# Start addresses of the split activations in a one-core transformer layer

## Chip, core and metric

One core of one Trainium2 chip. The metric is the device time of one execution in microseconds. The kernel before has a median of 2149.63 us over three runs (2149.45 to 2150.16).

## What is computed

The reference is one layer of a conformer-like network for a prompt of 256 tokens and a sample of 32 tokens, width 2048:

```python
def conformer_layer(x, mix, lp):
    x = x + 0.5 * swiglu(rmsnorm(x, lp['norm_ffn1']), lp['w_ffn1_in'], lp['w_ffn1_out'])
    y, state = mix(rmsnorm(x, lp['norm_mix']))
    x = x + y
    x = x + 0.5 * swiglu(rmsnorm(x, lp['norm_ffn2']), lp['w_ffn2_in'], lp['w_ffn2_out'])
    return rmsnorm(x, lp['norm_final']), state
```

`swiglu` projects to two times 43 x 128 columns, multiplies the silu of one half with the other, and projects back to 2048. `mix` projects to queries, keys, values and gates (`w_in`), runs a gated linear attention, a differential attention with a cache and an attention to a memory of 256 rows, and joins the three with `w_o`. All values are 32-bit floats, and so are the results: the new activations, the keys and values, and the state.

## The kernel before

All 288 tokens (256 and 32) are handled together and lie along the free dimension; channels lie on the 128 partitions. An activation of 2048 channels is thus 16 blocks of 128 x 288. The weights stream through the core once, in chunks of at most 512 KB, and each chunk is the stationary operand of TensorE.

To keep the precision of 32-bit floats with TensorE's faster 32-bit type (`float32r`), both operands are split. `split` has ScalarE (ACT) round a value to the fast type, the high part, and VectorE (DVE) subtract it, which leaves the low part. A product is then three matmuls: high weight by high activation, high weight by low activation, low weight by high activation. Weights are split chunk by chunk into the ring tiles wh and wl (`split_chunk`), four buffers each. Activations are split once per stage: the normed input into uh and ul (`prep_u`, `gsplit`), 16 blocks each, and the hidden values of the feed-forward into hh and hl, 22 blocks each, since a feed-forward is worked in two halves of 22 and 21 hidden blocks (`HALVES`).

`gemm` (line 271) is the loop that nearly all of the time goes to. For each chunk of up to four 128-row blocks it takes two column blocks of 128, and runs first all products with the high weight part, then all with the low part:

```python
for j in range(nk):
    xh, xl = xs(k + j)
    if part == 0:
        mm(o, wh[:, j, cs], xh, ci == 0 and j == 0, False)
        mm(o, wh[:, j, cs], xl, False, False)
    else:
        mm(o, wl[:, j, cs], xh, False, ci == nchunk - 1 and j == nk - 1)
```

So a chunk of four blocks is 24 matmuls, and the moving operand of each, `xh` or `xl`, is one block of 288 words per partition. All matmuls pass through one helper, line 83; which operand is meant is read from the tiles' names. `consume` (called in `gemm`) splits the weights three chunks ahead and starts loads six ahead, and between chunks `side` gives small pieces of attention work to the engines. The order on each engine is the order in which the program writes the instructions.

The stages in time: the memory's keys and values (`mem_group`, where the tiles mTh and mTl borrow the places of hh and hl), the first feed-forward (names ending in a), the projections of `mix` and the attentions, `w_o`, and the second feed-forward (names ending in b).

In the kernel before, the tiles uh, ul, hh, hl have rows of `NS` = 320 words, of which the first `NT` = 288 are used. 320 words are 1280 bytes, 5 x 256, so all blocks of a tile start at the same address modulo 256 bytes; in the layout of this program that is 32 for all four tiles. The blocks of wh and wl, 128 words wide, also all start at 32 modulo 256. The attention outputs that meet `w_o` (cdh, cdl, gch, gcl, from a pool of four-block tiles) have no padding: their blocks follow each other at 288 words, 1152 bytes, and so start at 32 and 160 in turn.

Of the kernel before, what the change touches and what calls it, by code (L numbers as in the profile page):

```python
# [11 lines left out]
F32R = mybir.dt.float32r  # L12
# [7 lines left out]
P = 128  # L20
NT = 288
NS = 320
D = 2048
KB = 16
# [16 lines left out]
def hybrid_step_kernel(  # L41
# [11 lines left out]
    def pool(name, bufs=1, **kw):  # L53
        return ctx.enter_context(tc.tile_pool(name=name, bufs=bufs, **kw))

    const = pool("const")
# [13 lines left out]
    def s1(name):  # L70
        return ps1.tile([P, 512], F32, tag="s1", name=name)
# [4 lines left out]
    def sm(name):  # L76
        return smp.tile([P, 32], F32, tag="sm", name=name)

    def sq2(name):
        return sqp.tile([P, 2, NT], F32, tag="sq", name=name)  # L80

    def mm(out, lhsT, rhs, start=True, stop=True):
        pe.matmul(out, lhsT, rhs, start=start, stop=stop)  # L83
# [5 lines left out]
    def tt(out, a, b, op):  # L89
        dve.tensor_tensor(out, a, b, op=op)  # L90

    def mul(out, a, b):
        dve.tensor_tensor(out, a, b, op=ALU.mult)  # L93
# [4 lines left out]
    def stt(out, a, s, b, op0, op1):  # L98
        dve.scalar_tensor_tensor(out, a, s, b, op0=op0, op1=op1)

    def split(hi, lo, src):
        act.copy(hi, src)  # L102
        tt(lo, src, hi.bitcast(F32), ALU.subtract)

    def gscale(out, src, g):
        act.activation(out, src, AF.Copy, scale=g)

    def gsplit(hi, lo, src, g):
        gscale(hi, src, g)
        stt(lo, src, g, hi.bitcast(F32), ALU.mult, ALU.subtract)  # L110

    def exp_tables():
        act.preload_act_table_set(ACT_SET)
# [11 lines left out]
    def kparts(n):  # L125
        return [4] * (n // 4) + ([n % 4] if n % 4 else [])
# [88 lines left out]
    def consume():  # L215
        i = nxt[2]
        nxt[2] += 1
        a = AHEAD if i >= 6 else 2
        splits_to(i + a)
        loads_to(i + a + 3)  # L220
        return chunks[i][2], halved.pop(i)
# [3 lines left out]
    class Thread:  # L225
        def __init__(self, lag):
            self.q, self.lag, self.ready = deque(), lag, 0
# [32 lines left out]
    def side(most=2):  # L260
        for t in threads:
            if most and t.can():
                t.step()
                most -= 1

    def need(mark):
        while mark not in done:
            t = next(t for t in threads if any(x[1] == mark for x in t.q))
            t.step()

    def gemm(nchunk, xs, nblk=2):

        ps = psm.tile([P, 2, 512], F32, tag="m", name=f"m{nxt[2]}")
        k = 0
        for ci in range(nchunk):
            nk, (wh, wl) = consume()
            for part in range(2):
                for b in range(nblk):
                    cs = slice(b * P, (b + 1) * P)
                    o = ps[:, b, :NT]  # L280
# [7 lines that stand above are left out]
            k += nk  # L288
            if ci < nchunk - 1:
                side()  # L290
        return ps

    fstack = [None]

    def open_ffn():
# [53 lines left out]
    x_res = const.tile([P, KB, NT], F32, name="x_res")  # L349
    G = const.tile([P, G_N], F32, name="G")  # L350
    lam = const.tile([P, 1], F32, name="lam")
    uh = const.tile([P, KB, NS], F32R, name="uh")[:, :, :NT]
    ul = const.tile([P, KB, NS], F32R, name="ul")[:, :, :NT]
    acc = const.tile([P, NT], F32, name="acc")
    dkc = const.tile([P, 4, P], F32, name="dkc")
    dvc = const.tile([P, 512], F32, name="dvc")
# [7 lines left out]
    def gcol(i):  # L364
        return G[:, i:i + 1]
# [28 lines left out]
    def prep_sq(i):  # L394

        sq = sq2("sq")
        act.activation(sq, x_res[:, 2 * i:2 * i + 2, :], AF.Square)
        if fresh[0]:
            tt(acc, sq[:, 0, :], sq[:, 1, :], ALU.add)
            fresh[0] = False  # L400
        else:
            for j in range(2):
                tt(acc, acc, sq[:, j, :], ALU.add)

    def prep_u(i, g0):
        for b in (2 * i, 2 * i + 1):
            gsplit(uh[:, b, :], ul[:, b, :], x_res[:, b, :], gcol(g0 + b))

    def later_R(name):

# [6 lines left out]
    def Rb(n):  # L417
        return acc.unsqueeze(1).to_broadcast([P, n, NT])


    hp = fstack[0][1]
    mTh = hp.tile([P, 22, NS], F32R, tag="hh", name="mTh").rearrange("p a t -> p (a t)")[:, :4096]
    mTl = hp.tile([P, 22, NS], F32R, tag="hl", name="mTl").rearrange("p a t -> p (a t)")[:, :4096]
    mTh = mTh.rearrange("p (k m) -> p k m", m=256)
    mTl = mTl.rearrange("p (k m) -> p k m", m=256)
    mss = sm("mss")
    mrs = sm("mrs")

# [25 lines left out]
    def x_step(i):  # L454
        half, o = divmod(i, 4)
        ps = s2(f"xt{i}")
        for b in range(2):
            for t, (t0, n) in enumerate(TT):
                c = (2 * o + b) * P
                tr(ps[:, b, t0:t0 + P], xtiles[half, t][:, c:c + P])  # L460
        act.copy(x_res[:, 2 * i:2 * i + 2, :], ps[:, :, :NT])
        prep_u(i, G_F1)
        prep_sq(i)
# [230 lines left out]
    def ffn(tag, mark, g_next, final=False):  # L694
        hp, fp = fstack[0][1], fstack[0][2]

        def ft(nm, bufs):
            return fp.tile([P, 2, NT], F32, tag=nm, bufs=bufs, name=f"{nm}_{tag}")

        def u(k):  # L700
            return uh[:, k, :], ul[:, k, :]

        for half, (a, b) in enumerate(HALVES):
            hh = hp.tile([P, 22, NS], F32R, tag="hh", name=f"hh{tag}{half}")[:, :, :NT]
            hl = hp.tile([P, 22, NS], F32R, tag="hl", name=f"hl{tag}{half}")[:, :, :NT]
            f = a
            while f < b:
                pair = f + 1 < b
                n = 2 if pair else 1
                ps = gemm(4, u)  # L710
                need(mark)
                gs = ft("gs", 1)[:, :n]
                sg = ft("sg", 2)[:, :n]
                mul(gs, ps[:, :n, :NT], Rb(n))
                act.activation(gs, gs, AF.Silu)  # L715
                mul(sg, gs, Rb(n))
                if pair:
                    side()
                    ps = gemm(4, u)
                    up = ps[:, :2, :NT]  # L720
                else:
                    up = ps[:, 1:2, :NT]
                hm = ft("hm", 1)[:, :n]
                mul(hm, up, sg)
                split(hh[:, f - a:f - a + n, :], hl[:, f - a:f - a + n, :], hm)
                f += n
                if f == NF:
                    exp_tables()
                side()
            for g in range(8):  # L730
                ps = gemm(len(kparts(b - a)), lambda k: (hh[:, k, :], hl[:, k, :]))
                xs = x_res[:, 2 * g:2 * g + 2, :]
                if final and half == 1 and g == 7:
                    sq = sq2("sql")
                    last_sq.append(sq)
                    for j in range(2):
                        stt(xs[:, j, :], ps[:, j, :NT], 0.5, xs[:, j, :], ALU.mult, ALU.add)
                        act.activation(sq[:, j, :], xs[:, j, :], AF.Square)
                else:
                    stt(xs, ps[:, :, :NT], 0.5, xs, ALU.mult, ALU.add)  # L740
                if half == 1:
                    if final:
                        final_pair(g)
                    else:
                        prep_sq(g)
                        prep_u(g, g_next)
                side()

    ffn("a", "R_ffn1", G_MIX)
    need("prep")  # L750
    close_ffn()
# [422 lines left out]
    later_R("mix")  # L1174

    def u(k):
        return uh[:, k, :], ul[:, k, :]

    for kind, c0, g in MIX:
        if kind == "glr":  # L1180
            ps = psm.tile([P, 2, 512], F32, tag="m", name="mglr")
# [9 lines left out]
            side()  # L1191
            continue
        ps = gemm(4, u)
        need("R_mix")
        pv = ps[:, :, :NT]
# [65 lines left out]
    for half in range(2):  # L1261
        if half == 1:
            need("gla")
        for g in range(8):
            if half == 0:
                ps = gemm(2, lambda k: (cdh[:, k, :], cdl[:, k, :]))
            else:
                ps = gemm(2, lambda k: tuple(a[:, k % 4, :] for a in M["cat", k // 4]))
# [45 lines left out]

    yr = sm("yr")
    ffn("b", "R_ffn2", None, final=True)
    ps = s1("yss")
    for j in range(2):
# [6 lines left out]
    for k, (hf, t, parts) in enumerate(((0, 0, 2), (0, 1, 1), (0, 2, 1), (1, 2, 1), (1, 0, 1), (1, 1, 1))):  # L1325
        rows = slice(0, P) if t < 2 else slice(96, P)
        dst = y_prompt[0, t * P:(t + 1) * P] if t < 2 else y_sample[0]
        n = 1024 // parts
# [66 lines left out]
```

## Time and profile before

| what | value |
|---|---|
| median of 3 runs | 2149.63 us (2149.45 to 2150.16) |
| the profiled execution's own time | 2149.8 us |
| its span, first to last instruction | 2148.0 us |
| mean granted TensorE clock | 0.996 |
| TensorE busy | 2133.2 us, 16,014 matmuls |
| VectorE, ScalarE, GpSimd busy | 1116.0, 866.0, 2.6 us |
| read from HBM | 345.59 MB |

The profile is one execution, taken by the hardware profiler. The page lists busy time by engine, the span in 40 slices, the DMA queues, the chain of work that ended last, and groups of like instructions with their count, busy time and mean duration. PE stands for TensorE's matmuls, PEld for its weight loads, DVE for VectorE, ACT for ScalarE. Matmuls are pipelined: one has a duration of about 294 ns in the records while the next starts long before it ends, so their pace is read from start to start, in the timeline or by counting them in a window.

### The profile page before, as it was taken

What the parts mean: (1) busy time and instruction counts of PE and PEld (TensorE: products, weight loads), DVE (VectorE), ACT (ScalarE), POOL (GpSimd) and SP (SyncE); (2) the same over time, 40 slices, a digit from 0 to 9 for tenths busy, and PEclk for the clock granted to TensorE, in tenths of its full rate; (3) what the DMA queues carried; (4) which work ended last, traced back from release to release, by engine and by line L of the source; (5) the groups of instructions that cost most, each with busy time, mean ns of one, the idle gap of its engine ahead of it and who ended that gap; (6) DMA issues with size and microseconds to landing.
All of it is one profiled execution on the core that took longest, in us unless ns stands there. A gap on an engine that the chain in (4) does not pass through costs nothing.

```text
span 2148.0 us, 37526 instructions
## 1 busy us (share of the span) xinstructions
PE 2133.2 (99%) x16014; PEld 2105.7 (98%) x16014; DVE 1116.0 (52%) x1318; ACT 866.0 (40%) x1113; POOL 2.6 (0%) x8
## 2 busy tenths in 40 slices
PE   9999999999999999999999999999999999999997
PEld 7999999999999999999999999999999999999997
DVE  6754444444554455554665666544544445445443
ACT  7644333333333344433544345333333333333443
POOL 0000000000000000000000000000000000000000
PEclk9999999999999999999999999999999999999998
DMA  8566555555555545554455345555555555555553
GB/s 261 177 182 189 178 166 173 171 163 172 162 168 170 166 155 166 178 151 135 121 147 154 121 151 166 168 170 168 162 167 165 169 167 166 171 167 163 160 161 117
DMA packets 351555, 353.75 MB, mean 165 GB/s; under 512 B 14112, under 2 KB 343324, under 8 KB 351388
## 3 DMA queue, kind: packets, MB, share of 16 engines
q1 hardware_dynamic: 351388, 351.36, 53.6%
q8 instruction: 125, 2.05, 0.4%
q14 instruction: 42, 0.34, 0.0%
HBM read 345.59 MB, written 5.64 MB: 164 GB/s over the span
## 4 chain that ended last, share of the span: by engine, by line
PE 98%; DMA 0%; ACT 0%; DVE 0%; SPq 0%; issue 0%; ACTq 0%; DVEq 0%
PE m L83 93%; PE mm L83 2%; PE go L83 1%; DMA ws<-in_w_mem_kv_dram 0%; PE do L83 0%; PE mo L83 0%; PE xt L87 0%; PE gK L83 0%; PE msc L83 0%; PE dsc L83 0%; PE sums L83 0%; PE yt L87 0%; PE mt L87 0%; PE hs_dq L83 0%; PE hs_mq L83 0%; PE gKs L83 0%
## 5 line engine op out<-in xcount | busy, mean ns | idle before, releaser
L90 DVE TENSOR_TENSOR wl<-ws,wh 128x1024 fp32r<-128x1024 f32 (+2 forms) x665 | 781.5, 1190 | 665.1 <-ACT wh L102 635.7
L102 ACT CAST wh<-ws 128x1024 fp32r<-128x1024 f32 (+2 forms) x665 | 665.3, 1018 | 658.6 <-PE m L83 527.5
L83 PE MATMUL m<-uh,wh 128*128 128x288 f32 x3392 | 913.5, 297 | 0.0
L83 PE MATMUL m<-ul,wh 128*128 128x288 f32 x3392 | 908.2, 294 | 0.0
L83 PEld LDWEIGHTS m<-uh,wh 128*128 128x128 f32 x3392 | 637.9, 188 | 2.9 <-issue 1.8
L83 PEld LDWEIGHTS m<-ul,wh 128*128 128x128 f32 x3392 | 638.5, 188 | 0.3
L83 PE MATMUL m<-uh,wl 128*128 128x288 f32 x3392 | 515.8, 294 | 0.0
L83 PEld LDWEIGHTS m<-uh,wl 128*128 128x128 f32 x3392 | 470.8, 188 | 0.0
L83 PE MATMUL m<-hhb,wh 128*128 128x288 f32 x688 | 184.7, 295 | 0.0
L83 PE MATMUL m<-hha,wh 128*128 128x288 f32 x688 | 184.3, 295 | 0.0
L83 PE MATMUL m<-hlb,wh 128*128 128x288 f32 x688 | 184.2, 294 | 0.0
L83 PE MATMUL m<-hla,wh 128*128 128x288 f32 x688 | 184.0, 293 | 0.0
L83 PEld LDWEIGHTS m<-hla,wh 128*128 128x128 f32 x688 | 129.1, 188 | 0.0
L83 PEld LDWEIGHTS m<-hlb,wh 128*128 128x128 f32 x688 | 129.1, 188 | 0.0
L83 PEld LDWEIGHTS m<-hhb,wh 128*128 128x128 f32 x688 | 129.1, 188 | 0.0
L83 PEld LDWEIGHTS m<-hha,wh 128*128 128x128 f32 x688 | 129.0, 188 | 0.0
L83 PE MATMUL m<-hha,wl 128*128 128x288 f32 x688 | 106.2, 294 | 0.0
L83 PE MATMUL m<-hhb,wl 128*128 128x288 f32 x688 | 106.1, 294 | 0.0
L83 PEld LDWEIGHTS m<-hha,wl 128*128 128x128 f32 x688 | 96.0, 188 | 0.0
L83 PEld LDWEIGHTS m<-hhb,wl 128*128 128x128 f32 x688 | 95.9, 188 | 0.0
L715 ACT ACTIVATE gs_b<-gs_b 128x576 f32<-128x576 f32 (+1 forms) x22 | 14.8, 674 | 84.6 <-DVE gs_b L93 84.6
L102 ACT CAST hhb<-hm_b 128x576 fp32r<-128x576 f32 (+1 forms) x22 | 14.6, 663 | 83.2 <-DVE hm_b L93 83.2
(282 smaller groups left out, 1180.1 us busy)
## 6 DMA issues: line engine op xcount, KB each, us to landing
ws<-in_w_ffn_in_dram SPq DMA_DIRECT2D x336, 512.0 KB, 4.2
ws<-in_w_ffn_out_dram SPq DMA_DIRECT2D x160, 512.0 KB, 3.5
ws<-in_w_in_dram SPq DMA_DIRECT2D x80, 512.0 KB, 3.7
ws<-in_w_o_dram SPq DMA_DIRECT2D x32, 512.0 KB, 3.5
ws<-in_w_mem_kv_dram SPq DMA_DIRECT2D x15, 512.0 KB, 5.7
ws<-in_w_ffn_out_dram SPq DMA_DIRECT2D x16, 256.0 KB, 2.8
ws<-in_w_ffn_in_dram SPq DMA_DIRECT2D x16, 256.0 KB, 3.2
x<-in_x_prompt_dram SPq DMA_DIRECT2D x4, 512.0 KB, 7.3
```

The lines of the kernel that those rows point to most:

```text
L83: pe.matmul(out, lhsT, rhs, start=start, stop=stop)
L90: dve.tensor_tensor(out, a, b, op=op)
L102: act.copy(hi, src)
L715: act.activation(gs, gs, AF.Silu)
```

## The change

The rows stay 320 words apart, but every group of four blocks is shifted by a number of words of its own. A small class holds a tile with 64 spare words and a list of shifts, one for each four blocks: block k starts at k x 320 + shift[k // 4]. `at` gives one block, `pair` two neighbours of one group.

uh and ul become one tile of 32 blocks, in which four high blocks are followed by the four low blocks of the same rows. Both get the same shift: 1, 2, 58 and 62 words for blocks 0 to 3, 4 to 7, 8 to 11 and 12 to 15. On top of the tile's own start, 32 modulo 256 bytes, that is 36, 40, 8 and 24. hh and hl stay two tiles, with shifts of 20, 28, 36, 44, 48 and 52 words for their six groups (the last has two blocks, or one in the second half): 112, 144, 176, 208, 224 and 240. Each tile grows by 64 words, 256 bytes. mTh and mTl keep the start of their tile.

```diff
+    class Blocks:
+
+        def __init__(self, pool_, n, shifts, name, **kw):
+            self.t, self.s = pool_.tile([P, n * NS + 64], F32R, name=name, **kw), shifts
+
+        def at(self, k):
+            o = k * NS + self.s[k // 4]
+            return self.t[:, o:o + NT]
+
+        def pair(self, k, n):
+            assert k // 4 == (k + n - 1) // 4
+            o = k * NS + self.s[k // 4]
+            return self.t[:, o:o + n * NT + (n - 1) * (NS - NT)] if n == 1 else \
+                self.t[:, o:o + n * NS].rearrange("p (k t) -> p k t", t=NS)[:, :, :NT]
+
+    U_SHIFT, H_SHIFT = (1, 2, 58, 62), (20, 28, 36, 44, 48, 52)
...
-    uh = const.tile([P, KB, NS], F32R, name="uh")[:, :, :NT]
-    ul = const.tile([P, KB, NS], F32R, name="ul")[:, :, :NT]
+    uhl = Blocks(const, 2 * KB, [a for a in U_SHIFT for _ in range(2)], "uhl")
...
-            gsplit(uh[:, b, :], ul[:, b, :], x_res[:, b, :], gcol(g0 + b))
+            gsplit(uhl.at(b + b // 4 * 4), uhl.at(b + b // 4 * 4 + 4), x_res[:, b, :], gcol(g0 + b))
...
-    mTh = hp.tile([P, 22, NS], F32R, tag="hh", name="mTh").rearrange("p a t -> p (a t)")[:, :4096]
-    mTl = hp.tile([P, 22, NS], F32R, tag="hl", name="mTl").rearrange("p a t -> p (a t)")[:, :4096]
-    mTh = mTh.rearrange("p (k m) -> p k m", m=256)
-    mTl = mTl.rearrange("p (k m) -> p k m", m=256)
+    mTh, mTl = (Blocks(hp, 22, H_SHIFT, f"mT{c}", tag=f"h{c}").t[:, :4096].rearrange("p (k m) -> p k m", m=256)
+                for c in "hl")
...
         def u(k):
-            return uh[:, k, :], ul[:, k, :]
+            return uhl.at(k + k // 4 * 4), uhl.at(k + k // 4 * 4 + 4)
...
-            hh = hp.tile([P, 22, NS], F32R, tag="hh", name=f"hh{tag}{half}")[:, :, :NT]
-            hl = hp.tile([P, 22, NS], F32R, tag="hl", name=f"hl{tag}{half}")[:, :, :NT]
+            hh, hl = (Blocks(hp, 22, H_SHIFT, f"h{c}{tag}{half}", tag=f"h{c}") for c in "hl")
...
-                split(hh[:, f - a:f - a + n, :], hl[:, f - a:f - a + n, :], hm)
+                split(hh.pair(f - a, n), hl.pair(f - a, n), hm if n > 1 else hm[:, 0, :])
...
-                ps = gemm(len(kparts(b - a)), lambda k: (hh[:, k, :], hl[:, k, :]))
+                ps = gemm(len(kparts(b - a)), lambda k: (hh.at(k), hl.at(k)))
```

The function u of the projections of `mix` changes as the one shown.

More of the change, by code (lines that the diff above doesn't have):

```diff
@@ L1176, in u @@
     def u(k):
-        return uh[:, k, :], ul[:, k, :]
+        return uhl.at(k + k // 4 * 4), uhl.at(k + k // 4 * 4 + 4)
     for kind, c0, g in MIX:
```

## The prediction

> **What bounds the kernel now.** I read the page's busy table first, then the slices, the chain, the groups, and at the end single matmuls in the timeline. The first three:
>
> ```profile
> span 2148.0 us, 37526 instructions
> PE 2133.2 (99%) x16014; PEld 2105.7 (98%) x16014; DVE 1116.0 (52%) x1318; ACT 866.0 (40%) x1113; POOL 2.6 (0%) x8
> ...
> PEclk9999999999999999999999999999999999999998
> DMA  8566555555555545554455345555555555555553
> ...
> PE 98%; DMA 0%; ACT 0%; DVE 0%; SPq 0%; issue 0%; ACTq 0%; DVEq 0%
> PE m L83 93%; PE mm L83 2%; PE go L83 1%; DMA ws<-in_w_mem_kv_dram 0%; PE do L83 0%; PE mo L83 0%; PE xt L87 0%; PE gK L83 0%; PE msc L83 0%; PE dsc L83 0%; PE sums L83 0%; PE yt L87 0%; PE mt L87 0%; PE hs_dq L83 0%; PE hs_mq L83 0%; PE gKs L83 0%
> ```
>
> TensorE is busy 99% at the full granted clock, and 93% of the chain that ended last are its matmuls into m, the products of gemm. Nothing else is near: DMA engines are half idle, DVE and ACT too. So the time is the number of these matmuls times the distance from the start of one to the start of the next. Busy time per matmul (294 ns) is no measure of that, since matmuls overlap. The counts are in the groups:
>
> ```profile
> L83 PE MATMUL m<-uh,wh 128*128 128x288 f32 x3392 | 913.5, 297 | 0.0
> L83 PE MATMUL m<-ul,wh 128*128 128x288 f32 x3392 | 908.2, 294 | 0.0
> ...
> L83 PE MATMUL m<-uh,wl 128*128 128x288 f32 x3392 | 515.8, 294 | 0.0
> ...
> L83 PE MATMUL m<-hhb,wh 128*128 128x288 f32 x688 | 184.7, 295 | 0.0
> L83 PE MATMUL m<-hha,wh 128*128 128x288 f32 x688 | 184.3, 295 | 0.0
> ```
>
> Three groups of 3392 read u: 10,176 matmuls. The h side has six groups of 688, two of them shown (hha, hhb with wh and with wl; hla, hlb with wh): 4,128. Together 14,304 matmuls, all of one shape, and the change moves the start address of the moving operand of every one of them.
>
> **The distance between matmuls.** In the timeline of TensorE, columns are start and duration in us. First a stretch of the second feed-forward, where all moving blocks start at 32 modulo 256 bytes (the kernel's stride of 320 words is 5 x 256 bytes):
>
> ```profile
> 1799.90 0.29 PE L83 MATMUL m<-uh,wh 128*128 128x288 f32 x1
> 1800.03 0.29 PE L83 MATMUL m<-ul,wh 128*128 128x288 f32 x1
> 1800.16 0.30 PE L83 MATMUL m<-uh,wh 128*128 128x288 f32 x1
> 1800.30 0.29 PE L83 MATMUL m<-ul,wh 128*128 128x288 f32 x1
> 1800.43 0.29 PE L83 MATMUL m<-uh,wh 128*128 128x288 f32 x1
> 1800.56 0.29 PE L83 MATMUL m<-ul,wh 128*128 128x288 f32 x1
> 1800.69 0.30 PE L83 MATMUL m<-uh,wh 128*128 128x288 f32 x1
> ...
> 1801.48 0.29 PE L83 MATMUL m<-uh,wh 128*128 128x288 f32 x1
> ```
>
> Twelve starts lie between 1799.90 and 1801.48: 1.58 / 12 = 131.7 ns. The steps are not even: three of about 130.5 ns and a fourth, after the matmul shown with 0.30, near 135 (0.14 in these rounded rows, once from 1800.16 to 1800.30). This pattern of four repeats through whole stages.
>
> The kernel holds one experiment on the address already. The tiles gch and cdh, the attention outputs that meet w_o, are not padded: their blocks are 288 words, 1152 = 4.5 x 256 bytes apart, so every other block starts at 160 instead of 32. Their timeline, one chunk of 24 products:
>
> ```profile
> 1261.57 0.29 PE L83 MATMUL m<-gch,wh 128*128 128x288 f32 x1
> 1261.70 0.29 PE L83 MATMUL m<-gcl,wh 128*128 128x288 f32 x1
> 1261.83 0.30 PE L83 MATMUL m<-gch,wh 128*128 128x288 f32 x1
> 1261.97 0.29 PE L83 MATMUL m<-gcl,wh 128*128 128x288 f32 x1
> ...
> 1263.71 1.23 PE L83 MATMUL m<-gch,wl 128*128 128x288 f32 x8
> 1264.77 0.29 PE L83 MATMUL m<-gch,wh 128*128 128x288 f32 x1
> ```
>
> From the first row to the last are 24 steps in 3.20 us: 133.3 ns. A count over longer windows (columns: the stretch, TensorE busy with the number of matmuls into m, granted clock, DMA share, GB/s) says the same:
>
> ```profile
> 1245.00:1310.00 65.00, 65.00 (x490) 1.00 0.54 170
> 600.00:665.00 65.00, 65.00 (x496) 1.00 0.56 168
> ...
> 1800.00:1865.00 65.00, 65.00 (x496) 1.00 0.57 172
> ```
>
> 490 against 496 rows in 65 us, at one clock and one DMA share. About two rows are under way when a window opens, so 65 / 488 = 133.2 and 65 / 494 = 131.6 ns. Half the blocks of the slower window start at 32 like all of the faster. If the two addresses simply add, a block at 160 costs 2 x (133.33 - 131.67) = 3.33 ns more per matmul, 135.0 ns. That is an estimate: the trace doesn't separate the address 160 from the alternation.
>
> **The change part by part.** No instruction is added or removed: the same matmuls, copies and subtractions work on shifted tiles. Tiles behind the enlarged ones move by exactly 256 bytes, so their address modulo 256, the weights' among them (32, as the moving blocks now), stays. What changes is:
>
> 1. The h blocks, 4,128 matmuls, go to 112, 144, 176, 208, 224 and 240. Blocks 0 to 3 of each half are 4 x 2 halves x 2 stages x 48 products = 768 matmuls, so are the next four groups, and the last (two blocks and one) has 288. No row shows 112 or 144. The nearest are 32 (no cost) and 160 (3.33 ns), which bound each from both sides. I take the cost as growing in line with the distance from 32 round the circle of 256 bytes, with 128 bytes costing 3.33 ns, 0.026 ns a byte. The distances are 80, 112, 112, 80, 64 and 48: 2.08, 2.92, 2.92, 2.08, 1.67 and 1.25 ns. 768 x 11.67 + 288 x 1.25 = 9.3 us.
> 2. The u blocks, 10,176 matmuls, go to 36, 40, 8 and 24: distances 4, 8, 24, 8, mean 11 bytes, 0.29 ns by the same line. 2.9 us. They are nearest to the row at 32, so I take them close to no cost; but this part has 71% of the matmuls and no row at an address that is not a multiple of 32, so it is the largest unknown.
> 3. uh and ul become one tile. ACT writes the high parts and DVE the low parts of the same blocks as before, by the groups with shapes kept apart:
>
> ```profile
> L106 ACT ACTIVATE uh<-x_res,G 128x288 fp32r<-128x288 f32 x48 | 22.9, 525 | 0.3
> L99 DVE SCALAR_TENSOR_TENSOR ul<-x_res,G,uh 128x288 fp32r<-128x288 f32 x48 | 22.6, 512 | 0.2 <-ACT uh L106 0.2
> ```
>
>    If one tile brought a false wait between them, ACT (40% busy) and DVE (52%) have the room, and only the first product of the stages that follow could be late. I cost it at nothing; without cover it is the two writes, 1 us, at three stage starts, 3 us.
>
> Sum: 9.3 + 2.9 = 12.2 us. Against the profiled execution's own time, 2149.8 us (its span of 2148.0 and 1.8 around it; the median of the runs is 2149.63, 0.2 below): **2162 us**.
>
> Bounds for the 14,304 matmuls: with the steps all at the shortest the pattern of four holds, 130 ns, 1.67 x 14,304 = 23.9 us less, 2126 us. With all at the price of 160, 3.33 x 14,304 = 47.7 us more, 2197 us.
>
> **The rivals.**
>
> *Faster: the meeting of two reads goes away.* Now the moving blocks and the weights both start at 32, and the weight load of the next matmul runs under each matmul:
>
> ```profile
> 1345.12 0.30 PE L83 MATMUL m<-uh,wh 128*128 128x288 f32 x1
> 1345.12 0.19 PEld L83 LDWEIGHTS m<-ul,wh 128*128 128x128 f32 x1
> ...
> 1345.26 0.29 PE L83 MATMUL m<-ul,wh 128*128 128x288 f32 x1
> 1345.26 0.19 PEld L83 LDWEIGHTS m<-uh,wh 128*128 128x128 f32 x1
> ```
>
> If the long fourth step (135 against 130.6) is a collision of these two reads at equal addresses, any shift may remove it: 4.4 / 4 = 1.1 ns for each of 14,304, 15.7 us, **2134 us**. For it: the addresses are equal, the loads start within 10 ns of the matmul. Against it: at 160, away from the weights' 32, the long step is longer, not gone. It decides as soon as u, with 71%, sheds its fourth step, whatever h does.
>
> [...]
>
> [...]
>
> *No change.* If the 1.67 ns of gch and cdh come from the alternation between blocks 128 bytes apart and not from the place, an address that is constant over a chunk costs nothing, and a switch happens once in 24 matmuls: **2150 us**. The two cannot be told apart in this trace.
>
> [...]
>
> **How the numbers follow.** Forecast (h by its distance, u nearly free): 0.40. Broken fetches: 0.17. Faster: 0.28, since 32 was never chosen against other addresses as far as the trace shows and u may lie on either side of it. No change: 0.15. So slower by over 0.2% (4.3 us, about what a measurement of this kernel tells from none) has 0.57, same 0.15, faster 0.28. The range that holds 8 in 10 reaches from just below the faster rival to just past the broken fetches: 2130 to 2180 us. The likeliest case by itself, u between -0.5 and +0.8 ns and h between 4 and 13.8 us (all at 160), is 2149 to 2172 us.
>
> **What would show it.** In the profile after, the start-to-start distance of the four u groups and six h groups within one stage, and how often the long step comes. Right: h's chunks in feed-forward out at 133 to 135 ns, dearest at 144 and 176, u's chunks within 0.7 ns of 131.7. The faster rival: u's chunks near 130.6 with even steps. [...] No change: all at 131.7. ACT, DVE, DMA and the counts of instructions must stay as they are; new waits of TensorE for uhl at a stage's start would show part 3 wrong. The prediction fails if u moves by more than 1 ns either way, as 10 us hang on each.

## The result, and the profile after

The changed kernel takes 2178.12 us (median of four runs, 2177.53 to 2178.99) against 2149.54 us for the kernel before, beside it on the same chip. The ratio is 1.0133 with a 95% interval of 1.0120 to 1.0145: slower, by 28.6 us. The profiled execution took 2177.53 us, 27.7 us more than the one before. The forecast was 2162.

The page of the changed kernel, first its span and busy table, then the granted clock, then the chain that ended last by engine, then two groups that read u (busy us, mean ns of one, idle before):

```profile
span 2175.8 us, 37526 instructions
PE 2159.8 (99%) x16014; PEld 2132.8 (98%) x16014; DVE 1116.4 (51%) x1318; ACT 866.0 (40%) x1113; POOL 2.6 (0%) x8
...
PEclk9999999999999999999999999999999999999999
...
PE 99%; DMA 0%; ACT 0%; DVE 0%; SPq 0%; issue 0%; ACTq 0%; DVEq 0%
...
L83 PE MATMUL m<-uhl,wh 128*128 128x288 f32 x6784 | 987.2, 298 | 0.0
...
L83 PE MATMUL m<-uhl,wl 128*128 128x288 f32 x3392 | 524.6, 297 | 0.0
```

The instruction counts of all engines are those of before, DVE and ACT are as busy in us as they were, the clock is full, and no idle time stands before the products. TensorE alone got longer: 2159.8 - 2133.2 = 26.6 us more busy time, in the same 16,014 matmuls. Nothing waits for anything new; the same matmuls start further apart. Matmuls into m in 65 us (columns: the stretch, busy time and count, granted clock, DMA share, GB/s):

```profile
600.00:665.00 65.00, 65.00 (x486) 1.00 0.55 163
...
1800.00:1865.00 65.00, 65.00 (x486) 1.00 0.55 163
```

Both stretches held 496 before. With the two rows that are under way when a window opens left out, 65 / 484 = 134.3 ns, where it was 65 / 494 = 131.6.

The timeline shows which blocks pay. Each pair of rows below is one chunk of 24 products over four blocks of u, at 40, 8 and 24 modulo 256; the last row is the next chunk's first. Columns are start and duration in us:

```profile
342.82 2.30 PE L83 MATMUL m<-uhl,wh 128*128 128x288 f32 x16
344.97 1.23 PE L83 MATMUL m<-uhl,wl 128*128 128x288 f32 x8
346.03 2.35 PE L83 MATMUL m<-uhl,wh 128*128 128x288 f32 x16
348.22 1.26 PE L83 MATMUL m<-uhl,wl 128*128 128x288 f32 x8
349.31 2.28 PE L83 MATMUL m<-uhl,wh 128*128 128x288 f32 x16
351.43 1.22 PE L83 MATMUL m<-uhl,wl 128*128 128x288 f32 x8
352.49 0.30 PE L83 MATMUL m<-hha,wh 128*128 128x288 f32 x1
```

From chunk start to chunk start these are 3.21, 3.28 and 3.18 us: 133.8, 136.7 and 132.5 ns for a matmul. And four chunks of h, each by its first row, at 112, 144, 176 and 208:

```profile
1717.34 0.29 PE L83 MATMUL m<-hhb,wh 128*128 128x288 f32 x1
...
1720.48 0.29 PE L83 MATMUL m<-hhb,wh 128*128 128x288 f32 x1
...
1723.70 0.30 PE L83 MATMUL m<-hhb,wh 128*128 128x288 f32 x1
...
1726.83 0.30 PE L83 MATMUL m<-hhb,wh 128*128 128x288 f32 x1
...
1729.99 0.29 PE L83 MATMUL m<-hhb,wh 128*128 128x288 f32 x1
```

3.14, 3.22, 3.13 and 3.16 us: 130.8, 134.2, 130.4 and 131.7 ns. So 176, which is far from 32, is faster than 32 itself was, and 8, which is near it, is the dearest of all.

In what follows the **pace** of an address is the distance from the start of one matmul to the next, worked out from the starts of single matmuls in the trace, the median over its chunks. Before, all blocks of u and h had 131.67 ns. The changed kernel:

| blocks | address mod 256 | pace, ns | matmuls | against 131.67, us |
|---|---|---|---|---|
| u 0-3 | 36 | 135.33 | 2544 | +9.3 |
| u 4-7 | 40 | 133.67 | 2544 | +5.1 |
| u 8-11 | 8 | 136.54 | 2544 | +12.4 |
| u 12-15 | 24 | 132.58 | 2544 | +2.3 |
| h 0-3 | 112 | 131.17 | 768 | -0.4 |
| h 4-7 | 144 | 133.12 | 768 | +1.1 |
| h 8-11 | 176 | 130.38 | 768 | -1.0 |
| h 12-15 | 208 | 131.42 | 768 | -0.2 |
| h 16-19 | 224 | 133.12 | 768 | +1.1 |
| h 20-21 | 240 | 133.30 | 288 | +0.5 |

u adds 29.1 us and h 1.1 us, together 30.2 where 27.7 to 28.6 were measured. The change is paid for by u. At 144 the chunks have two paces, 133.1 ns in 18 of them and 134.1 in 14; the table has the median, which falls on the lower.

### The profile page after: what moved, and what is told of

Same layout as the page of the kernel before. It is cut to its first block, busy times and chain, and to the rows that moved or that the text cites. A ratio compares the mean times of both kernels' runs of the same rounds, so it can differ in the third digit from the quotient of the medians.

```text
span 2175.8 us, 37526 instructions
## 1 busy us (share of the span) xinstructions
PE 2159.8 (99%) x16014; PEld 2132.8 (98%) x16014; DVE 1116.4 (51%) x1318; ACT 866.0 (40%) x1113; POOL 2.6 (0%) x8
## 4 chain that ended last, share of the span: by engine, by line
PE 99%; DMA 0%; ACT 0%; DVE 0%; SPq 0%; issue 0%; ACTq 0%; DVEq 0%
PE m L83 93%; PE mm L83 2%; PE go L83 1%; DMA ws<-in_w_mem_kv_dram 0%; PE do L83 0%; PE mo L83 0%; PE xt L87 0%; PE gK L83 0%; PE msc L83 0%; PE dsc L83 0%; PE sums L83 0%; PE yt L87 0%; PE hs_dq L83 0%; PE mt L87 0%; PE hs_mq L83 0%; PE gKs L83 0%
## 5 line engine op out<-in xcount | busy, mean ns | idle before, releaser
L83 PE MATMUL m<-uhl,wh 128*128 128x288 f32 x6784 | 987.2, 298 | 0.0
L83 PEld LDWEIGHTS m<-uhl,wh 128*128 128x128 f32 x6784 | 936.6, 190 | 3.2 <-issue 1.8
L83 PE MATMUL m<-uhl,wl 128*128 128x288 f32 x3392 | 524.6, 297 | 0.0
L83 PEld LDWEIGHTS m<-uhl,wl 128*128 128x128 f32 x3392 | 479.6, 190 | 0.0
L102 ACT CAST hha<-hm_a 128x576 fp32r<-128x576 f32 (+1 forms) x22 | 14.6, 663 | 83.8 <-DVE hm_a L93 83.8
L727 ACT ACTIVATE gs_a<-gs_a 128x576 f32<-128x576 f32 (+1 forms) x22 | 14.8, 674 | 81.1 <-DVE gs_a L93 81.1
```

## The experiments

Nine kernels ran, one of them twice, all made from the changed one by other lists of shifts, and one by moving the weights as well. An address is always meant modulo 256 bytes; the weights start at 32 unless the text says otherwise.

### u alone, h alone

The first kernel shifts only u (h stays at 32, in the enlarged tiles); the second shifts only h (u at 32, in its joint tile).

```diff
 # e1_u_only
-    U_SHIFT, H_SHIFT = (1, 2, 58, 62), (20, 28, 36, 44, 48, 52)
+    U_SHIFT, H_SHIFT = (1, 2, 58, 62), (0, 0, 0, 0, 0, 0)
 # e2_h_only
-    U_SHIFT, H_SHIFT = (1, 2, 58, 62), (20, 28, 36, 44, 48, 52)
+    U_SHIFT, H_SHIFT = (0, 0, 0, 0), (20, 28, 36, 44, 48, 52)
```

> The u blocks alone are shifted (36, 40, 8, 24), the h blocks stay at 32 modulo 256 bytes. Theory place (each start address has a price of its own per matmul, whatever the operand is): u's 10,176 matmuls bring nearly the whole loss, 27 to 29 us, about 2177 us. My forecast (the price grows with the distance from 32): 2.9 us, 2152 us. Theory one tile (the loss comes from uh and ul sharing a tile, not from addresses): the loss comes here too, but as waits of TensorE for uhl, with the pace of matmuls at 131.7 ns.

> The h blocks alone are shifted (112 to 240), u stays at 32 but in the joint tile. Theory place: the six groups keep the paces of the changed kernel (131.2, 133.1, 130.4, 131.4, 133.1, 133.5 ns), together about 1 us, 2150 to 2151 us. My forecast: 9.3 us, 2159 us. Theory one tile: 2177 us, since the joint tile is here as well.

u alone took 2176.98 us against 2149.69 before, ratio 1.0127 (1.0112 to 1.0142): +27.3 us. h alone took 2150.95, ratio 1.0006 (0.9996 to 1.0015): +1.3 us, the same as before within what can be measured. The two differences add up to the 28.6 of the change. In the same two stretches, first u alone, then h alone:

```profile
600.00:665.00 65.00, 65.00 (x486) 1.00 0.53 162
...
1800.00:1865.00 65.00, 65.00 (x485) 1.00 0.53 163
```

```profile
600.00:665.00 65.00, 65.00 (x496) 1.00 0.56 169
...
1800.00:1865.00 65.00, 65.00 (x496) 1.00 0.56 170
```

With u shifted alone the count is that of the changed kernel; with u at 32 inside the joint tile it is that of before. So the joint tile costs nothing, and the paces hardly depend on where the other operand's blocks lie: u had 135.33, 133.67, 136.54 and 132.58 ns as in the changed kernel, and h in the second kernel 131.17, 133.62, 130.38, 131.54, 133.12 and 133.25. Only 144 differs, and 133.62 is no pace that occurs: 16 chunks have 133.1 and 16 have 134.1 ns, where the changed kernel had 18 and 14.

### All blocks at the fastest address so far

176 had the lowest pace of the ten. If the pace goes with the address, all blocks can have it.

```diff
-    U_SHIFT, H_SHIFT = (1, 2, 58, 62), (20, 28, 36, 44, 48, 52)
+    U_SHIFT, H_SHIFT = (36, 36, 36, 36), (36, 36, 36, 36, 36, 36)
```

> All u and h blocks start at 176, where the changed kernel's h group had the shortest pace, 130.4 ns. Theory place: 14,304 matmuls at 1.29 ns less than 131.67, 18 us less than before, 2131 us, and a pace of 130.4 ns on u too. My forecast by distance: 2.9 ns more each, 2191 us. If the gain at 176 belonged to h or to the mixture with other addresses: near 2149 us.

2139.08 us (2137.33 to 2139.36), ratio 0.9950 (0.9935 to 0.9964): faster than before by 10.6 us, so u and h follow the address alike. But it is not as fast as the pace on h said. Two chunks of u in this kernel, one early, one later, each from its first row to the first of the next:

```profile
104.49 2.24 PE L83 MATMUL m<-uhl,wh 128*128 128x288 f32 x16
106.57 1.20 PE L83 MATMUL m<-uhl,wl 128*128 128x288 f32 x8
107.61 0.55 PE L83 MATMUL m<-uhl,wh 128*128 128x288 f32 x3
...
601.93 2.26 PE L83 MATMUL m<-uhl,wh 128*128 128x288 f32 x16
604.02 1.21 PE L83 MATMUL m<-uhl,wl 128*128 128x288 f32 x8
605.08 0.42 PE L83 MATMUL m<-uhl,wh 128*128 128x288 f32 x2
```

3.12 us and 3.15 us: 130.0 and 131.2 ns at one address. The trace falls into one of two steady cycles of steps; most chunks have the slower: the windows at 600 and at 1800 hold 498 rows in 65 us, 65 / 496 = 131.0 ns. In this kernel every block of u and h has the same address, and no chunk changes from one cycle to the other unless other work of TensorE comes in between. So an address doesn't fix the pace alone; what ran before has a part in which cycle it settles in.

### Two surveys: all multiples of 4

Each stage (first feed-forward, mix, second feed-forward) and each half of h gets a list of its own, so that one kernel holds 36 addresses and the two together all 64 multiples of 4. The reads follow the stage:

```diff
-        def at(self, k):
-            o = k * NS + self.s[k // 4]
+        def at(self, k, st=None):
+            o = k * NS + (self.s[k // 4] if st is None else U_SHIFT[st][k // 8])
...
-    U_SHIFT, H_SHIFT = (1, 2, 58, 62), (20, 28, 36, 44, 48, 52)
 # s1
+    U_SHIFT = (0, 4, 8, 12), (16, 20, 24, 28), (32, 36, 40, 44)
+    H_SHIFT = {('a', 0): (48, 50, 52, 56, 60, 62), ('a', 1): (1, 2, 3, 5, 6, 7),
+               ('b', 0): (9, 10, 11, 13, 14, 15), ('b', 1): (17, 18, 19, 21, 22, 23)}
 # s2
+    U_SHIFT = (25, 26, 27, 29), (30, 31, 33, 34), (35, 37, 38, 39)
+    H_SHIFT = {('a', 0): (41, 42, 43, 45, 46, 47), ('a', 1): (49, 51, 53, 54, 55, 57),
+               ('b', 0): (58, 59, 61, 62, 63, 63), ('b', 1): (0, 12, 20, 28, 36, 44)}
```

> A survey: u and h blocks get other addresses in each stage and half, so that one execution shows the pace at 36 addresses: all with a shift of 4 words times 0 to 15 (u has 0 to 44, h 48 to 60), and between them words 1, 2, 3, 5, 6, 7, 9, 10, 11, 13, 14, 15, 17, 18, 19, 21, 22, 23, 50 and 62 (h). Theory place: u at 112, 144, 176, 208 (words 20, 28, 36, 44) paces like h did: 131.2, 133.1, 130.4, 131.4 ns, and h at 36, 40 and 24 like u did: 135.3, 133.7, 132.6 ns. [...] My forecast by distance: highest, 135, at 160 (word 32), falling to both sides.

> The survey's second half, the other words: u at 25, 26, 27, 29, 30, 31, 33, 34, 35, 37, 38, 39 (132 to 188 bytes), h at the words from 41 to 63 that are no multiple of 4, and h again at 0, 12, 20, 28, 36, 44. Theory place: the last six repeat what the first half and the changed kernel showed (131.7, 132.8, 131.2, 133.1, 130.4, 131.4 ns, within 0.3); word 58 (8 bytes) shows 136.5 on h, as on u. Theory history (the pace is that of a cycle which the chunk before decides too, so that one address can have several): the repeats differ by up to 2 ns.

They took 2161.82 and 2178.41 us, one run each. These totals are of little use, being mixtures; what counts is the pace of each address, in ns. Steps in which other work held TensorE up (over 170 ns) are left out. Most of them, from the survey that held it:

```
on u, s1:  32 131.75   48 131.79   64 133.33   80 132.83
          160 133.54  176 130.12  192 133.25  208 131.42
on u, s2: 132 135.96  136 133.58  140 133.33  148 133.54
          164 133.98  172 132.58  180 139.33  184 133.21  188 130.17
on h, s1:   0 133.25   16 132.04   24 133.17   36 133.25   40 134.46   44 131.25
           72 131.50   76 130.21   92 132.67  108 133.35  116 136.21  240 133.33
on h, s2:   8 133.79   28 129.98   32 131.67  112 131.15  176 130.04  204 130.00
          212 133.25  220 129.79  228 135.71  236 130.17  244 136.33  252 131.12
```

There is no line in it, and no distance: 180 and 188 lie 8 bytes apart and stand at 139.33 and 130.17, the dearest and one of the fastest. Being a multiple of 16 doesn't make an address fast: 64, 160, 192, 224 and 240 have 133.1 to 133.5, and 28, 76, 188, 204 and 220, multiples of 4 alone, about 130. The remainder is not without weight, though. Over all 64 addresses, 16 for each remainder, those that are 0, 4, 8 and 12 bytes past a multiple of 16 average 132.5, 134.9, 133.8 and 131.2 ns, and the five fast ones just named are all 12 past. Within one remainder the paces still spread by 3.6 ns or more.

The expectation that a place has its price held for five of the six addresses repeated at the end of survey 2, within 0.4 ns; 144 shows 134.3 for 133.1, the second of its two paces. Two addresses differ by 2 ns or more from the changed kernel, where other chunks ran before them: 8 (136.54 there on u, 133.79 here on h) and 36 (135.33 and 133.25). The changed kernel itself shows both paces of 8: 18 of its 106 chunks there ran at 133.2 to 133.8 ns, 82 at 136.5. That is the second thing that 176 showed. Most addresses of h have eight chunks here, so their paces are the less certain.

### The weights moved as well

Survey 1 again, with the rings of the split weights at 160 in place of 32 and the moving blocks where they were modulo 256. "Nothing else moves", as the expectation below has it, is not quite so: by the pads shown in the diff, the buffers in which the unsplit weights land, and the tiles that follow uhl in its pool, move by 64 bytes modulo 256. The products of `gemm` read none of them.

```diff
+    pool("pada").tile([P, 16], F32, name="pada")
     wrp = pool("wrp", 4)
+    pool("padb").tile([P, 32], F32, name="padb")
...
-        def __init__(self, pool_, n, shifts, name, **kw):
-            self.t, self.s = pool_.tile([P, n * NS + 64], F32R, name=name, **kw), shifts
+        def __init__(self, pool_, n, shifts, name, pad=64, **kw):
+            self.t, self.s = pool_.tile([P, n * NS + pad], F32R, name=name, **kw), shifts
...
-    uhl = Blocks(const, 2 * KB, [a for a in U_SHIFT for _ in range(2)], "uhl")
+    uhl = Blocks(const, 2 * KB, None, "uhl", pad=16)
```

> The first survey once more, with all split weights at 160 in place of 32 modulo 256 bytes; nothing else moves. Theory distance to the weights (the price belongs to the difference of the two addresses): the curve moves along by 128 bytes, so u at 160, 176, 192, 208 shows what 32, 48, 64, 80 showed (131.7, 131.8, 133.3, 132.8 ns), and u at 32, 48, 64, 80 shows what 160, 176, 192, 208 showed (133.5, 130.1, 133.3, 131.4). Theory place of the moving operand alone: every address as in the first survey, u at 176 again at 130.1, at 160 at 133.5.

2165.44 us in one run. If the price were the place's, u at 32 would keep 131.75 ns and u at 160 its 133.54. They changed places. The second feed-forward of survey 1 (weights at 32), u at 160, 176 and the start of 192:

```profile
1459.39 2.30 PE L83 MATMUL m<-uhl,wh 128*128 128x288 f32 x16
1461.52 1.23 PE L83 MATMUL m<-uhl,wl 128*128 128x288 f32 x8
1462.59 2.25 PE L83 MATMUL m<-uhl,wh 128*128 128x288 f32 x16
1464.67 1.20 PE L83 MATMUL m<-uhl,wl 128*128 128x288 f32 x8
1465.71 2.29 PE L83 MATMUL m<-uhl,wh 128*128 128x288 f32 x16
```

The first feed-forward of the kernel with the weights at 160, u at 32, 48 and the start of 64:

```profile
153.93 2.30 PE L85 MATMUL m<-uhl,wh 128*128 128x288 f32 x16
156.06 1.23 PE L85 MATMUL m<-uhl,wl 128*128 128x288 f32 x8
157.13 2.25 PE L85 MATMUL m<-uhl,wh 128*128 128x288 f32 x16
159.21 1.20 PE L85 MATMUL m<-uhl,wl 128*128 128x288 f32 x8
160.25 2.29 PE L85 MATMUL m<-uhl,wh 128*128 128x288 f32 x16
```

Row for row the durations are equal, and the chunks last 3.20 and 3.12 us in both. In both, moving block minus weights is 128, 144 and 160 bytes. The other way round, u at 160 and 176 under weights at 160 (0 and 16 apart):

```profile
1462.53 2.27 PE L85 MATMUL m<-uhl,wh 128*128 128x288 f32 x16
...
1465.69 2.27 PE L85 MATMUL m<-uhl,wh 128*128 128x288 f32 x16
...
1468.85 2.30 PE L85 MATMUL m<-uhl,wh 128*128 128x288 f32 x16
```

3.16 us each, 131.7 ns, the pace of 32 and 48 in survey 1. By paces, all eight u addresses of the two feed-forwards agree pairwise within 0.05 ns at the same difference:

```
moving - weights    0       16      32      48      128     144     160     176
weights at  32    131.75  131.79  133.33  132.83  133.54  130.12  133.25  131.42
weights at 160    131.75  131.79  133.33  132.83  133.54  130.12  133.25  131.42
```

The rest of the kernel says the same. Over all 36 addresses, the pace lies on average 0.14 ns from the surveys' at the same difference and 1.45 ns from theirs at the same place; the 139.33 ns of u at 180 comes back on h at 52, 148 bytes from the weights in both. What counts is thus, beside what ran before, the difference between the two start addresses, not where the moving block lies. The weights were moved by 128 bytes alone, so a part that the place modulo 128 may have in it is not excluded.

### All at 76

76, that is 44 bytes past the weights' start, had the lowest pace of survey 1 on h among addresses with full chunks of 24 (60 and 124, with 6 matmuls a chunk, had 129.8 and 130.0), and it is no multiple of 16.

```diff
-    U_SHIFT, H_SHIFT = (1, 2, 58, 62), (20, 28, 36, 44, 48, 52)
+    U_SHIFT, H_SHIFT = (11, 11, 11, 11), (11, 11, 11, 11, 11, 11)
```

> All u and h blocks at 76, which in the survey had 130.2 ns and is a multiple of 4 but not of 16. Theory place: 14,304 matmuls at 1.46 ns less than at 32, 21 us less, about 2129 us. [...] Theory history: a pace other than in the survey, as 176 alone gave 131.1 ns in most chunks and 130.0 in some; anywhere from 2126 to 2150 us.

2125.02 us in one run against 2149.90 before. Timed in more runs:

> The version with all u and h blocks at 76, 44 bytes behind the weights' 32, timed in rounds against the kernel before. By its one profile 130.0 against 131.67 ns: 1.67 x 14,304 = 23.9 us less, 2125 to 2126 us. If that one execution was lucky in its cycle: up to 2135 us.

**2124.68 us** (2123.64 to 2125.27) against 2148.72, ratio 0.9886 (0.9869 to 0.9902): 24.0 us faster than the kernel before and 53 faster than the changed one, with the same instructions. Its page, the windows, and the starts of two chunks in the timeline:

```profile
span 2122.9 us, 37526 instructions
PE 2107.8 (99%) x16014; PEld 2080.7 (98%) x16014; DVE 1115.9 (53%) x1318; ACT 864.4 (41%) x1113; POOL 2.6 (0%) x8
```

```profile
600.00:665.00 65.00, 65.00 (x503) 1.00 0.56 171
...
1800.00:1865.00 65.00, 65.00 (x502) 1.00 0.53 162
```

```profile
349.35 0.29 PE L83 MATMUL m<-hha,wh 128*128 128x288 f32 x1
...
352.47 0.29 PE L83 MATMUL m<-hha,wh 128*128 128x288 f32 x1
```

3.12 / 24 = 130.0 ns. The long fourth step of before is gone: 99% of the steps of u and h lie between 127 and 133 ns. 1.67 ns x 14,304 matmuls = 23.9 us is the whole gain. It is also the lower bound that the prediction named, "with the steps all at the shortest".

### All at 160, all at 220

The first measures the price that the prediction had worked out from gch and cdh. The second is one more address with a pace near 130.

```diff
-    U_SHIFT, H_SHIFT = (1, 2, 58, 62), (20, 28, 36, 44, 48, 52)
 # e6_all_160
+    U_SHIFT, H_SHIFT = (32, 32, 32, 32), (32, 32, 32, 32, 32, 32)
 # e7_all_220
+    U_SHIFT, H_SHIFT = (47, 47, 47, 47), (47, 47, 47, 47, 47, 47)
```

> All u and h blocks at 160, 128 bytes from the weights: settles what the kernel before left open in gch and cdh, whose blocks lie at 32 and 160 in turn (133.3 ns). If addresses simply add, as my forecast took it: 135.0 ns, 47.7 us more, 2197 us. By the surveys' 133.5 ns at this distance: 1.87 x 14,304 = 26.8 us more, 2176 us. If the alternation was the cost: 131.7 ns, 2150 us.

> All u and h blocks at 220, 188 bytes behind the weights, the shortest pace of the surveys (129.8 ns in chunks of h between others). Theory distance: at most 130.0 ns when it is steady, 2122 to 2126 us. Theory history, that a pace between other addresses needn't last: 130.0 to 131.7 ns, 2126 to 2150 us.

160 took 2171.82 us and 220 took 2126.70, against 2148.72. The windows of 160, then of 220:

```profile
600.00:665.00 65.00, 65.00 (x489) 1.00 0.55 166
...
1800.00:1865.00 65.00, 65.00 (x490) 1.00 0.54 163
```

```profile
600.00:665.00 65.00, 65.00 (x502) 1.00 0.56 171
...
1800.00:1865.00 65.00, 65.00 (x503) 1.00 0.54 166
```

With all blocks at 160 the pace is 133.33 ns, 1.67 more than at 32: 23.9 us by the count of matmuls, 23.1 measured. gch and cdh, which alternate between 32 and 160, have the same 133.33. So the alternation did not average two prices: a mixture of 32 and 160 costs as much as 160 alone.

## Why the prediction was right or wrong

**What bounds the kernel: right.** The time is the number of matmuls into m times the distance from start to start. The totals of the experiments follow the paces: at 76, -24.0 us measured and -23.9 worked out; at 160, +23.1 and +23.9. Reading it from start to start, and not from the 294 ns of busy time, is what made the differences of 2 to 3 ns visible.

**Step 2, u "close to no cost": here the forecast failed.** It gave 0.29 ns a matmul, 2.9 us; the trace shows 2.86 ns, 29.1 us, and u alone measured +27.3. The sum missed by 16 us, and this step was short by 24 to 26. The reason given was nearness: 36, 40, 8 and 24 lie within 24 bytes of the one address with a known price. That took for granted that the price changes slowly with the address, for which the trace of before held two addresses and no third. The surveys show neighbours 8 bytes apart at 139.3 and 130.2 ns. The prediction had named this step its largest unknown, and a move of u by more than 1 ns as the sign of its failure.

**Step 1, h by its distance: wrong too, the other way.** 9.3 us were forecast, 1.1 worked out from the paces and 1.3 measured with h alone, which is no difference that can be told from none. "Dearest at 144 and 176" was half wrong: 176 was the fastest of all ten. Two errors lie under it. The line again; and its slope, since "if the two addresses simply add" made 160 cost 135.0 ns, where a kernel with all blocks there shows 133.33. The text called that an estimate which the trace doesn't separate, rightly; but then the upper bound of 47.7 us was no bound. 180, at 139.3 ns, lies above even that.

**Step 3, the joint tile: right.** It costs nothing, as the kernel that shifts h alone shows. The writes are as before, and TensorE's longest waits name nothing of u:

```profile
L106 ACT ACTIVATE uhl<-x_res,G 128x288 fp32r<-128x288 f32 x48 | 23.0, 526 | 0.3
...
L99 DVE SCALAR_TENSOR_TENSOR uhl<-x_res,G,uhl 128x288 fp32r<-128x288 f32 x48 | 22.6, 513 | 0.3 <-ACT uhl L106 0.3
```

```profile
PE mt L87 <- DMA mem<-in_mem_prompt_dram: 1.2, 1, 1.2
PE warm L83 <- DVE ones L358: 1.0, 1, 1.0
PE yss L83 <- ACT sql L750: 1.0, 1, 1.0
```

**The rivals.** No run shows *broken fetches*, to which the forecast gave 0.17 and the upper end of its range. What the runs show in its place: the chunks of u at 36, 40, 8 and 24 spread from 132.6 to 136.5 ns, and a start that is no multiple of 16 bytes is not slow by that alone, since all blocks at 76 run at 130.0 ns, below any multiple of 16 that was measured but 176, which reaches it in some chunks. The starts 12 bytes past a multiple of 16 are even faster on average than the multiples, 131.2 against 132.5 ns. *The meeting of two reads* had the right pair, the moving block against the weights, and its gain was there to be had: 24.0 us at 76, where it reckoned with 15.7. That two reads collide is not shown by this. But "any shift may remove it" was too much: 16 bytes apart is as slow as 0 (131.79 and 131.75 ns), 4 bytes and -24 bytes are slower (135.33 and 136.54), and 44 bytes is free of the long step (130.0). *No change* by alternation fell with the first result, since addresses constant over a chunk did cost. Its doubt, though, that 32 and 160 had been told apart, was sound.

That the side, slower, was right is luck, since the line that it rested on does not exist. The range of 2130 to 2180, held open by the rivals on both sides, does contain the 2178; the 2162 in the middle of it was not supported by the trace.

## What to carry to other kernels

Where TensorE never pauses (busy 99% here) and each matmul brings a new weight load (16,014 of each), the difference between the start addresses of the moving block and of the weights, modulo 256 bytes, is a parameter to be measured, like a tile size: here it was worth from -24 us to +28 us of 2150. It can't be interpolated from neighbours; one kernel with an address of its own for each group of blocks measures dozens at once, and the best must then be timed alone, since a pace can change with what ran before. Read the pace from start to start over a whole chunk.

## What the runs showed of the hardware

- The pace of a 128x128 by 128x288 fp32r matmul, with the next weights loading beneath it (188 ns a load in the trace of before), lies between 130.0 and 139.3 ns (129.8 in a few chunks of the surveys), at a granted clock of 1.00, with nothing changed but start addresses. Moving the weights by 128 bytes moved the paces of eight u addresses with them, within 0.05 ns.
- It isn't a smooth function of the difference, and no alignment alone decides it, though starts 12 bytes past a multiple of 16 average 131.2 ns and those 4 past 134.9: 44, 156, 172, 188 and 252 bytes past the weights' start reach 130.0 to 130.2 ns; 32, 128 and 160 have 133.3 to 133.5; 148 has 139.3.
- One address can have two steady cycles: at 176, 130.0 and 131.1 ns in one execution, at 144, 133.1 and 134.1.
- The rows of a plain 32-bit product are slower: in the trace of before the four rows of gz from 1072.72 us on, 128x128 by 128x288 and two for each product, take 403 to 406 ns each and start 242 ns apart, where those of gemm take 294 and start 131.67 apart.
- Open: why the pace goes with the difference of the two addresses, and what chooses between two cycles. Open too: whether the remainder by 16 that matters is the moving block's or the difference's, since the weights were only ever at multiples of 16. No run separated those. Nor was it tried to shift gch and cdh, whose 768 matmuls keep their addresses in the kernel at 76.
